# Interleaved column orders for the moving operand and the accumulator of 3,210 matmuls

## The chip, the cores and the metric

The kernel runs on one core of one Trainium2 chip. The metric is the device time of one execution in microseconds (us). TensorE (PE in the profile) multiplies, VectorE (DVE) and ScalarE (ACT) prepare operands and empty accumulators, GpSimd (POOL) and SyncE (SP) issue transfers. SBUF holds the operands, and PSUM holds the accumulators in banks of 512 fp32 columns for each of 128 partitions.

## The reference: one attention layer between two norms

With 256 rows and a width of 4096, one layer is computed:

```
h   = x + (o * silu(g)) @ w_out          # w_out: 4096 x 4096
q,k,v,g = split(rms_norm(x, norm_attn) @ w_in, 4)   # w_in: 4096 x 16384
o   = stick_breaking_attention(q, k, v)  # 32 heads of 128, strictly causal
out = rms_norm(h, final_norm)
```

All of it is float32. The weights have 5 x 4096 x 4096 values, 335 MB.

## The kernel before

**Arithmetic.** A float32 product is made of three matmuls in the type fp32r: each operand is cut into a rounded high part and the low rest, and `mm3` (L762) issues high by high, high by low and low by high into one accumulator. The rows (x, later the gated heads) are the stationary operand: 128 x 128 blocks `sh`/`sl` and, in the second projection, `oh`/`ol`. The weights are the moving operand: tiles `wh` (made by ACT) and `wl` (made by DVE), 512 columns wide, straight from the loaded tile `raw`.

**Units and steps.** The work is cut into 20 units, one after the other. Units 0 to 15 make the first projection, units 16 to 19 the second. Each unit goes through 16 steps along the width, and keeps seven accumulators b1 to b7 of 128 x 512 in seven PSUM banks. A unit from 1 on uses sums of blocks so that a step needs seven products in place of eight: steps 1, 3, 4, 6, 7, 9, 10, 12, 13 and 14 are such seven-product steps (`SEVEN`, L42, `SEVEN_PARTS`, L73), the other six have eight (`EIGHT_PARTS`, L79). So a unit has 10 x 7 + 6 x 8 = 118 products, or 354 matmuls. An eight-product step goes through the accumulators in the order 2, 2, 4, 4, 5, 5, 3, 3. The last step of a unit and the first of the next are both of that kind.

**Emptying the accumulators.** When a unit ends, `combine` (L658) makes the four results of the unit, in the tiles `qk_sb` and `gv_sb`. ACT copies b1 (L681, L682), DVE adds b6 and b7 (`add`, L665), then DVE adds b2, b4, b5 (twice) and b3 with a factor for each row (`add_scaled`, L668: one instruction SCALAR_TENSOR_TENSOR on 512 columns). An accumulator that has been read is given back (`nc.give`), and the next unit's first product into that bank waits for it.

**Order of the instructions.** The order on each engine is not written out by hand: the class `Plan` (L102) runs a model of the engines while the kernel is built. Each piece of work has a cost (`vector_ns`, L90) and a due time (`key`); a free engine takes the waiting piece with the lowest key. A changed cost can so move later instructions on all engines. `product` (L1185) calls `mm3` with the accumulator's bank and the weight's tile.

**Beside the projections** the heads of earlier units are computed: short matmuls `tr`, `z`, `o` between the products, and work on ACT and DVE.

Of the kernel before, what the change touches and what calls it, by code (L numbers as in the profile page):

```python
# [13 lines left out]
AF = mybir.ActivationFunctionType  # L14
ALU = mybir.AluOpType
# [4 lines left out]
P = 128  # L20
# [8 lines left out]
W = 2 * CW  # L29
# [27 lines left out]
ON_SCALAR = ((1, 3, 5), (1, 3))  # L57
AHEAD, SUMS_AHEAD = 4.0, 3.0
BLOCKS_LATER = 2


PLAIN = {"C11": 1, "C21": 6, "C12": 7, "C22": 3}
# [27 lines left out]
def vector_ns(n):  # L90
    return 67 + 1.0417 * n


def scalar_ns(n):
    return 98 + n / 1.2
# [142 lines left out]
def kernel(  # L238
# [10 lines left out]
    nc = Plan(tc)  # L249
    scale = 1.0 / math.sqrt(P)  # L250
# [49 lines left out]
    for g, (n, k) in enumerate(order):  # L300
        p = parts[n]
        b = p["u"], p["prods"][k][0]
# [8 lines left out]
    def place_at(u, s):  # L311

        return place_of[u + int(s // NS), step_at(u + int(s // NS), int(s % NS))]

    def soon(c=4.0):
        return nc.here + 1e3 * c


    def dve(emit, n, key=None, **kw):
        n = n if isinstance(n, tuple) else (n,)  # L320
        cost = sum(vector_ns(m) for m in n) + 122 * (len(n) - 1)
        return nc.work("vector", cost, emit, soon() if key is None else key, **kw)

    def act(emit, n, key=None, **kw):
        n = n if isinstance(n, tuple) else (n,)
        cost = sum(scalar_ns(m) for m in n) + 100 * (len(n) - 1)
        return nc.work("scalar", cost, emit, soon() if key is None else key, **kw)
# [14 lines left out]
    def together(*works):  # L342
        for w in works:
            nc.start(w)
# [164 lines left out]
    def blocks_of(i):  # L509
# [38 lines left out]
        nc.tell(("form", "s", i))  # L548
        later = place_at(0, i + BLOCKS_LATER)
        if not i:  # L550
# [19 lines left out]
    for k in range(WARM):  # L570
# [10 lines left out]
        out=bound, in_=bound, compare_op=ALU.is_gt, fill=0.0, base=0,  # L581
# [6 lines left out]
        out=tri_f, in_=tri_f, compare_op=ALU.is_ge, fill=0.0, base=0, pattern=[[-1, P]], channel_multiplier=1,  # L588
# [66 lines left out]
        yield dve(lambda: nc.vector.tensor_copy(neg_tri, tri_f), P)  # L655


    def combine(u, one, two, what):  # L658

        bank = ev[u]  # L660
        key = place_of[u + 1, 0]

        row = [rs["v"][:, t : t + 1] if u < OUT0 else 1.0 for t in range(NT)]

        def add(to, b, f, n):  # L665
            return dve(lambda: nc.vector.tensor_tensor(out=to, in0=bank[b], in1=f, op=ALU.add), W, key + n)

        def add_scaled(to, b, f, n, t):  # L668
            if u >= OUT0:
                return add(to, b, f, n)  # L670
            return dve(
                lambda: nc.vector.scalar_tensor_tensor(
                    out=to, in0=bank[b], scalar=row[t], in1=f, op0=ALU.mult, op1=ALU.add
                ),
                W, key + n,
            )

        def scaled(to, f, t):
            return act(lambda: nc.scalar.activation(to, f, AF.Copy, scale=row[t]), W, key - 2e3)

        yield act(lambda: nc.scalar.copy(two[:, 0, :], bank[1]), W, key - 2e3)  # L681
        yield scaled(one[:, 0, :], bank[1], 0)  # L682
        nc.give("b1")

        def early():
            yield nc.until(("full", u, 6))
            yield add(two[:, 0, :], 6, two[:, 0, :], 0)
            nc.give("b6")
            yield nc.until(("full", u, 7))
            yield add(two[:, 1, :], 7, two[:, 0, :], 0)  # L690
            nc.give("b7")
            yield scaled(one[:, 1, :], two[:, 1, :], 1)
            if u < OUT0:
                for t in (1, 0):
                    yield scaled(two[:, t, :], two[:, t, :], t)
            nc.tell(("early", u))

        def first_():
            yield nc.until(("full", u, 2))
            yield add_scaled(one[:, 0, :], 2, one[:, 0, :], 1, 0)  # L700
            nc.give("b2")
            yield nc.until(("full", u, 4), ("early", u))
            yield add_scaled(one[:, 1, :], 4, one[:, 1, :], 2, 1)
            nc.give("b4")
            nc.tell((what[0], u))

        def second():
            yield nc.until(("full", u, 5), ("early", u))
            for t in (1, 0):
                yield add_scaled(two[:, t, :], 5, two[:, t, :], 3, t)  # L710
            nc.give("b5")
            yield nc.until(("full", u, 3))
            yield add_scaled(two[:, 0, :], 3, two[:, 0, :], 4, 0)
            nc.give("b3")
            nc.tell((what[1], u))

        together(early(), first_(), second())

    def out_of(u):

        if u < 1:
            yield nc.until(("full", u, PLAIN["C11"]), "factor")
        else:
            yield nc.until(("full", u, 1))
        yield nc.take("one", "two")
        one = st["qk", u] = ap.tile([P, NT, W], F32, tag="one", name=f"qk_sb{u}")
        two = st["gv", u] = ap.tile([P, NT, W], F32, tag="two", name=f"gv_sb{u}")
        if u >= 1:
            yield from combine(u, one, two, ("qk", "gv"))
            return  # L730
        key = place_of[u + 1, 0] - 2e3
        for dst, col, t in ((one, 1, 0), (one, 1, 1), (two, 2, 0), (two, 2, 1)):
            b = PLAIN[f"C{t + 1}{col}"]
            yield nc.until(("full", u, b))
            yield act(
                lambda: nc.scalar.activation(dst[:, t, :], ev[u][b], AF.Copy, scale=rs["v"][:, t : t + 1]), W, key
            )
            nc.give(f"b{b}")
            if t == 1:
                nc.tell((("qk", "gv")[col - 1], u))  # L740


    st, ev = {}, {}
# [15 lines left out]
        nc.give("qkl")  # L759
        nc.tell(("gate", u))  # L760

    def mm3(out_, a, b, start, stop):  # L762

        (ah, al), (bh, bl) = a, b
        kw = dict(skip_group_check=True)
        nc.tensor.matmul(out_, ah, bh, start=start, stop=False, **kw)
        nc.tensor.matmul(out_, ah, bl, start=False, stop=False, **kw)
        nc.tensor.matmul(out_, al, bh, start=False, stop=stop, **kw)
# [195 lines left out]
    class Rows:  # L964


        def __init__(self, c):
            self.c = c

        def __getitem__(self, at_):  # L970
            return hs[self.c, at_[1]]
# [72 lines left out]
    def mixed_h(u, c):  # L1044
        yield nc.until(("full", u, 1))
        if c == NJ - 4:
            yield nc.take("raw", "gh")
        for k in range(2):
            new_h(c + k)
        yield from combine(u, Rows(c), Rows(c + 1), ("C1", "C2"))  # L1050
        yield nc.until(("C1", u), ("C2", u))
        nc.tell(("C", u))
# [132 lines left out]
    def product(n, k):  # L1185
        p = parts[n]
        b, f, c = p["prods"][k]
        h, l = forms[p["s"]]
        mm3(
            ev[p["u"]][b],  # L1190
            (h[:, PLACES[f], :], l[:, PLACES[f], :]),
            (wh[n][:, c, :], wl[n][:, c, :]),
            starts[p["u"], b] == (n, k),
            ends[p["u"], b] == (n, k),
        )

    def products():
        for g, (n, k) in enumerate(order):
            p = parts[n]
            u, s = p["u"], p["s"]  # L1200
            b, f, c = p["prods"][k]
            if u < 1:
                what = "s"
            elif u < OUT0:
                what = "n"
            elif u == OUT0:
                what = "o"
            else:
                what = "r" if u == LAST and s in EIGHT_LAST else "p"
            if starts[u, b] == (n, k):  # L1210
                yield nc.take(f"b{b}")
                ev.setdefault(u, {})[b] = acc.tile([P, W], F32, tag=f"b{b}", name=f"acc{u}_{b}")
            yield nc.until(("low", n, c), ("form", what, s), lead=nc.LEAD)
            yield nc.work(
                "tensor", PRODUCT, lambda: product(n, k), g * PRODUCT, after=lambda n=n, k=k: done(n, k), hold=False
            )
            nc.here = g * PRODUCT
# [59 lines left out]
```

## Time and profile before

| | |
|---|---|
| median of 2 runs | 1740.36 us (1740.18 to 1740.54) |
| span of the profiled execution, first to last instruction | 1738.8 us |
| between the span and the median, before the first and after the last instruction | 1.6 us |
| PE, DVE, ACT, POOL busy in the span | 1722.9, 1643.5, 1204.9, 335.5 us |
| granted TensorE clock, mean | 0.998 |
| matmuls of the projections | 7,149 |

A line of the profile names the engine, the operation, the tiles written and read (out<-in), shape and count, then the busy time, the mean duration of one, and how long the engine was idle before. All instructions go through one recording helper, so that every line is L121 and the tiles tell them apart. A matmul's duration overlaps the next one's; how fast a row of matmuls goes is read from the distance of their starts. A row of the view by windows gives, for a stretch of time, its length, the busy time of PE, of its weight load, of DVE, ACT and POOL, the granted clock, the share of the DMA engines and GB/s.

### The profile page before, as it was taken

How to read it: one execution, taken by the hardware profiler on the slowest of the kernel's cores; microseconds unless marked ns; L12 is line 12 of the kernel's file. 1: busy time of each engine (PE TensorE's matmuls, PEld its weight loads, DVE VectorE, ACT ScalarE, POOL GpSimd, SP SyncE). 2: the span in 40 equal slices, each digit the busy share in tenths (PEclk: the TensorE clock that was granted, in tenths of full speed). 3: DMA queues.
4: the chain of work that ended last, by engine and by line, in shares of the span. 5: the costliest groups of instructions: out<-in, count | busy, mean ns of one | idle time of the engine just before them, and what ended most of it. 6: DMA issues, size and time to landing. Idle time of an engine off the chain costs nothing.

```text
span 1738.8 us, 24830 instructions
## 1 busy us (share of the span) xinstructions
PE 1722.9 (99%) x7735; PEld 1412.5 (81%) x7735; DVE 1643.5 (95%) x2106; ACT 1204.9 (69%) x1640; POOL 335.5 (19%) x407
## 2 busy tenths in 40 slices
PE   9999999999999999999999999999999999999997
PEld 6888888888888888888888888888888888878885
DVE  8889999999999999999999999999999987999997
ACT  7976767676767676767676767676767675666655
POOL 0022222222222221212222222222222112221220
PEclk9999999999999999999999999999999999999999
DMA  9967788878787878787878787878787878788895
GB/s 363 297 191 227 229 231 226 230 229 236 224 234 223 240 216 238 217 251 208 255 206 255 206 256 198 257 203 259 198 256 203 269 245 265 230 268 251 233 303 191
DMA packets 249380, 413.79 MB, mean 238 GB/s; under 512 B 28128, under 2 KB 73440, under 8 KB 249248
## 3 DMA queue, kind: packets, MB, share of 16 engines
q1 hardware_dynamic: 194544, 354.24, 60.6%
q0 software_dynamic: 54416, 57.70, 20.2%
q8 instruction: 60, 0.98, 0.2%
q14 instruction: 72, 0.59, 0.1%
q10 hardware_dynamic: 288, 0.28, 0.0%
HBM read 403.98 MB, written 8.13 MB: 237 GB/s over the span
## 4 chain that ended last, share of the span: by engine, by line
PE 78%; DVE 12%; issue 6%; ACT 2%; DMA 2%; SPq 0%; DVEq 0%; ACTq 0%
PE acc L121 74%; DVE wl L121 8%; DVE raw L121 3%; PE z L121 2%; PE o L121 1%; ACT wh L121 1%; DMA raw<-in_w_in_dram 1%; PE tr L121 1%; DVE gv_sb L121 1%; DVE h L121 0%; DMA raw<-in_w_out_dram 0%; DMA grow<-in_gain_out_dram 0%; DVE qk_sb L121 0%; SPq L121 0%; ACT sq L121 0%
## 5 line engine op out<-in xcount | busy, mean ns | idle before, releaser
L121 ACT CAST wh<-raw 128x1024 fp32r<-128x1024 f32 (+1 forms) x995 | 922.0, 971 | 406.1 <-issue 180.0
L121 DVE TENSOR_TENSOR wl<-raw,wh 128x1024 fp32r<-128x1024 f32 (+1 forms) x995 | 1068.8, 1123 | 58.4 <-ACT wh L121 56.6
L121 PE MATMUL acc<-wh,sh 128*128 128x512 f32 x1898 | 755.6, 398 | 0.0
L121 PE MATMUL acc<-wl,sh 128*128 128x512 f32 x1898 | 740.0, 390 | 0.8 <-DVE wl L121 0.8
L121 PE MATMUL acc<-wh,sl 128*128 128x512 f32 x1898 | 740.5, 390 | 0.0
L121 POOL DMA_DIRECT2D raw<-in_w_in_dram x300 | 262.9, 988 | 1078.9 <-DMA raw<-in_w_in_dram 427.4
L121 PEld LDWEIGHTS acc<-wh,sl 128*128 128x128 f32 x1898 | 356.3, 188 | 75.8 <-DVE sl L121 0.4
L121 PEld LDWEIGHTS acc<-wl,sh 128*128 128x128 f32 x1898 | 357.0, 188 | 73.8 <-DVE wl L121 2.8
L121 PEld LDWEIGHTS acc<-wh,sh 128*128 128x128 f32 x1898 | 356.8, 188 | 70.7 <-ACT wh L121 0.6
L121 DVE TENSOR_TENSOR raw<-raw,raw 128x512 f32<-128x512 f32 x354 | 243.4, 687 | 6.9 <-DMA raw<-in_w_out_dram 1.2
L121 PE MATMUL acc<-wl,oh 128*128 128x512 f32 x485 | 189.7, 391 | 2.0 <-DVE wl L121 1.8
L121 PE MATMUL acc<-wh,oh 128*128 128x512 f32 x485 | 190.0, 392 | 0.0
L121 PE MATMUL acc<-wh,ol 128*128 128x512 f32 x485 | 188.9, 389 | 0.0
L121 DVE TENSOR_TENSOR raw<-raw 128x512 f32<-128x512 f32 x177 | 121.0, 684 | 0.0
L121 PEld LDWEIGHTS acc<-wl,oh 128*128 128x128 f32 x485 | 91.1, 188 | 23.8 <-DVE wl L121 5.3
L121 PEld LDWEIGHTS acc<-wh,oh 128*128 128x128 f32 x485 | 91.0, 188 | 19.2 <-DVE gv_sb L121 0.5
L121 PEld LDWEIGHTS acc<-wh,ol 128*128 128x128 f32 x485 | 91.0, 188 | 18.8
L121 POOL DMA_DIRECT2D raw<-in_w_out_dram x54 | 47.1, 968 | 185.9 <-DVE wl L121 58.9
L121 ACT ACTIVATE f<-f 128x384 f32<-128x384 f32 x96 | 50.5, 526 | 3.0
L121 ACT COPY qkT<-tr 128x512 f32<-128x512 f32 x32 | 18.6, 581 | 24.1 <-PE tr L121 24.1
L121 ACT CAST oh<-p 128x512 fp32r<-128x512 f32 (+3 forms) x46 | 20.9, 467 | 18.8 <-DVE p L121 13.2
L121 DVE SCALAR_TENSOR_TENSOR gv_sb<-acc,rin_v,gv_sb 128x512 f32<-128x512 f32 x45 | 33.4, 741 | 0.0
(91 smaller groups left out, 750.3 us busy)
## 6 DMA issues: line engine op xcount, KB each, us to landing
raw<-in_w_in_dram SPq DMA_DIRECT2D x1024, 256.0 KB, 4.5
raw<-in_w_out_dram SPq DMA_DIRECT2D x256, 256.0 KB, 4.3
raw<-in_w_in_dram POOLq DMA_DIRECT2D x300, 128.0 KB, 4.7
p<-spill POOLq DMA_DIRECT2D x28, 256.0 KB, 4.2
raw<-in_w_out_dram POOLq DMA_DIRECT2D x54, 128.0 KB, 5.1
xr<-in_x_dram SPq DMA_DIRECT2D x16, 256.0 KB, 4.8
xres<-in_x_dram SPq DMA_DIRECT2D x16, 256.0 KB, 5.6
out_dram<-h SPq DMA_DIRECT2D x16, 256.0 KB, 2.8
```

The source lines that it names most:

```text
L121: return self.tc.keep_in_program_order(getattr(self.engine, name)(*args, **kw))
```

## The change

`walked(t, (h, e))` reads the 512 columns of a tile as h blocks of runs of e neighbouring columns, and takes run 0 of every block, then run 1 of every block, and so on: (4, 2) goes through columns 0 1, 128 129, 256 257, 384 385, 2 3, 130 131 and so on. Between two runs lie 512 / h columns.

- In units 2, 3 and 4, six steps each (1, 3, 6, 9, 12, 14) take moving operand and accumulator in the same such order, so that every column ends where it ended before. `combine` of these units stays as it was.
- In units 6, 8, 10 and 12 only the accumulator is written in such an order; in units 7, 9, 11 and 13 only the moving operand is read in it. Then the columns stand in PSUM in another order than in the result, and `combine` puts them back: its copies and adds take one operand in the interleaved order, and `add_scaled` becomes four instructions on 128 columns (two on 256 for the order (16, 16)).

```diff
+WALKS = {
+    (u, s): w
+    for u, ws in {
+        2: ((4, 2), (8, 2), (16, 2), (32, 2), (64, 2), (128, 2)),
+        3: ((8, 4), (16, 4), (32, 4), (64, 4), (4, 8), (8, 8)),
+        4: ((16, 8), (32, 8), (4, 32), (8, 32), (32, 4), (64, 4)),
+    }.items()
+    for s, w in zip((1, 3, 6, 9, 12, 14), ws)
+}
+OUT_WALKS = {6: (32, 4), 8: (8, 16), 10: (16, 16), 12: (64, 2)}
+IN_WALKS = {7: (32, 4), 9: (8, 16), 11: (16, 16), 13: (64, 2)}
+def walked(t, w):
+    return t.rearrange("p (h i e) -> p i h e", h=w[0], e=w[1]) if w else t
+def cut_like(t, w):
+    i = W // w[0] // w[1] if w else 1
+    return t.rearrange("p (i h e) -> p i h e", i=i, e=w[1]) if w else t
...
+    class Banks:
...
+        def __getitem__(self, b):
+            u = self.u
+            ow, iw = OUT_WALKS.get(u), IN_WALKS.get(u)
+            return walked(ev[u][b], ow) if ow else cut_like(ev[u][b], iw)
     def combine(u, one, two, what):
-        bank = ev[u]
+        ow, iw = OUT_WALKS.get(u), IN_WALKS.get(u)
+        bank = Banks(u)
+        side = lambda t: walked(t, iw) if iw else cut_like(t, ow)
...
         def add_scaled(to, b, f, n, t):
             if u >= OUT0:
                 return add(to, b, f, n)
-            return dve(
-                lambda: nc.vector.scalar_tensor_tensor(
-                    out=to, in0=bank[b], scalar=row[t], in1=f, op0=ALU.mult, op1=ALU.add
-                ),
-                W, key + n,
-            )
+            if not ow and not iw:
...
+            def pieces():
+                T, B, F = side(to), bank[b], side(f)
+                for i in range(T.shape[1]):
+                    nc.vector.scalar_tensor_tensor(
+                        out=T[:, i], in0=B[:, i], scalar=row[t], in1=F[:, i], op0=ALU.mult, op1=ALU.add
+                    )
+            return dve(pieces, (P,) * 4, key + n)
...
-    def mm3(out_, a, b, start, stop):
+    def mm3(out_, a, b, start, stop, to=None, by=None):
         (ah, al), (bh, bl) = a, b
+        out_, bh, bl = walked(out_, to), walked(bh, by), walked(bl, by)
+        if to and not by:
+            bh, bl = cut_like(bh, to), cut_like(bl, to)
+        if by and not to:
+            out_ = cut_like(out_, by)
```

`product` hands `mm3` the order of its unit and step for the accumulator and for the moving operand.

More of the change, by code (lines that the diff above doesn't have):

```diff
@@ L655, in constants, with __init__ @@
         yield dve(lambda: nc.vector.tensor_copy(neg_tri, tri_f), P)
+    class Banks:
+        def __init__(self, u):
+            self.u = u
+        def __getitem__(self, b):
+            u = self.u
+            ow, iw = OUT_WALKS.get(u), IN_WALKS.get(u)
+            return walked(ev[u][b], ow) if ow else cut_like(ev[u][b], iw)
     def combine(u, one, two, what):
-        bank = ev[u]
+        ow, iw = OUT_WALKS.get(u), IN_WALKS.get(u)
+        bank = Banks(u)
+        side = lambda t: walked(t, iw) if iw else cut_like(t, ow)
         key = place_of[u + 1, 0]
@@ L665, in add @@
         def add(to, b, f, n):
-            return dve(lambda: nc.vector.tensor_tensor(out=to, in0=bank[b], in1=f, op=ALU.add), W, key + n)
+            return dve(lambda: nc.vector.tensor_tensor(out=side(to), in0=bank[b], in1=side(f), op=ALU.add), W, key + n)
         def add_scaled(to, b, f, n, t):
@@ L670, in add_scaled, with scaled @@
                 return add(to, b, f, n)
-            return dve(
-                lambda: nc.vector.scalar_tensor_tensor(
-                    out=to, in0=bank[b], scalar=row[t], in1=f, op0=ALU.mult, op1=ALU.add
-                ),
-                W, key + n,
-            )
[L678 to L682, printed above, removed]
+            if not ow and not iw:
+                return dve(
+                    lambda: nc.vector.scalar_tensor_tensor(
+                        out=to, in0=bank[b], scalar=row[t], in1=f, op0=ALU.mult, op1=ALU.add
+                    ),
+                    W, key + n,
+                )
[4 more added lines that the diff above has]
+                        out=T[:, i], in0=B[:, i], scalar=row[t], in1=F[:, i], op0=ALU.mult, op1=ALU.add
+                    )
+            return dve(pieces, (P,) * 4, key + n)
+        def scaled(to, f, t, side=lambda t: t):
+            return act(lambda: nc.scalar.activation(side(to), f, AF.Copy, scale=row[t]), W, key - 2e3)
+        yield act(lambda: nc.scalar.copy(side(two[:, 0, :]), bank[1]), W, key - 2e3)
+        yield scaled(one[:, 0, :], bank[1], 0, side)
         nc.give("b1")
@@ L1194, in product @@
             ends[p["u"], b] == (n, k),
+            WALKS.get((p["u"], p["s"]), OUT_WALKS.get(p["u"])),
+            WALKS.get((p["u"], p["s"]), IN_WALKS.get(p["u"])),
         )
```

## The prediction

> **What bounds the kernel now.** I read the page's head first, then the PE groups by shape, the timeline of PE, and the view by windows.
>
> ```profile
> span 1738.8 us, 24830 instructions
> PE 1722.9 (99%) x7735; PEld 1412.5 (81%) x7735; DVE 1643.5 (95%) x2106; ACT 1204.9 (69%) x1640; POOL 335.5 (19%) x407
> ```
>
> ```profile
> L121 PE MATMUL acc<-wh,sh 128*128 128x512 f32 x1898 | 755.6, 398 | 0.0
> L121 PE MATMUL acc<-wh,sl 128*128 128x512 f32 x1898 | 740.5, 390 | 0.0
> ...
> L121 PE MATMUL acc<-wh,oh 128*128 128x512 f32 x485 | 190.0, 392 | 0.0
> ...
> L121 PE MATMUL warm<-idle 128*128 128x512 bf16 x10 | 4.4, 628 | 1.3 <-DVE idle L121 1.3
> ```
>
> There are three products with the same counts for `sh` and three for `oh`: 3 x 1898 + 3 x 485 = 7149 projection matmuls. Their real pace is the distance of starts; 34 distances lie between these two rows:
>
> ```profile
> 704.11 0.39 PE L121 MATMUL acc<-wl,sh 128*128 128x512 f32 x1
> ...
> 711.81 0.39 PE L121 MATMUL acc<-wh,sl 128*128 128x512 f32 x1
> ```
>
> (711.81 - 704.11) / 34 = 0.2265 us a matmul. 7149 x 0.2265 = 1619 us of the span's 1738.8 us. The windows below are units 2, 6, 11 and 13, then the sum over eleven windows: units 2, 3, 4 and 6 to 13, those that the change touches.
>
> ```profile
> core 0: us, PE busy (x) PEld busy (x) DVE busy (x) ACT busy (x) POOL busy (x), PEclk, DMA share, GB/s
> 181.15:267.23 86.08, 86.08 (x392) 70.80 (x391) 82.96 (x102) 60.45 (x80) 18.15 (x22) 1.00 0.81 229
> ...
> 525.47:611.61 86.14, 86.14 (x391) 70.82 (x390) 82.98 (x103) 60.41 (x80) 17.95 (x22) 1.00 0.82 230
> ...
> 956.24:1042.34 86.10, 86.10 (x392) 70.81 (x390) 82.97 (x102) 60.46 (x80) 18.01 (x21) 1.00 0.80 229
> ...
> 1128.45:1214.54 86.09, 86.09 (x391) 70.80 (x390) 82.94 (x102) 61.41 (x81) 19.12 (x23) 1.00 0.82 233
> sum 947.33, PE 947.33 PEld 778.88 DVE 912.59 ACT 665.06 POOL 198.53; mean PE 86.12 PEld 70.81 DVE 82.96 ACT 60.46 POOL 18.05
> ```
>
> PE is busy 947.33 of 947.33 us at the full granted clock. So a nanosecond on each matmul there lengthens the kernel, one for one. The second thing to see is DVE: 82.96 of 86.12 us a unit, only 3.16 us idle.
>
> **Part 1, the matmuls.** The order of the columns changes no count and no size. Both-sided: 18 steps x 7 products x 3 = 378 matmuls. Accumulator alone: 4 units x 354 = 1416. Moving operand alone: 1416. Together 3210 of 7149. Runs of two columns are read from the moving operand in unit 2 (6 x 21 = 126) and unit 13 (354), 480 matmuls; written to the accumulator in unit 2 and unit 12, also 480; together 834.
>
> No matmul of the trace has an interleaved operand, so the price is bounded. Lower end: nothing, the 0.2265 us above. Upper end: the slowest row on 512 columns is the warm-up's 628 ns against 390, 238 ns more, about one more pass over the columns (512 columns take 0.2265 us). Below nothing the trace gives no faster row on 512 columns, and a faster PE would soon wait for DVE: 3.16 us idle a unit at most. I take nothing: pairs and longer runs stay neighbours, the pace of one column in 0.44 ns is all that the rows show, and no row shows a penalty for an address. That is the weakest step, and the range holds the rest.
>
> [...]
>
> **Part 2, DVE in units 6 to 13.** Five `add_scaled` a unit are cut into pieces.
>
> ```profile
> L121 DVE TENSOR_TENSOR wl<-raw,wh 128x512 fp32r<-128x512 f32 x179 | 122.4, 684 | 1.2 <-ACT wh L121 1.2
> L121 DVE SCALAR_TENSOR_TENSOR gv_sb<-acc,rin_v,gv_sb 128x512 f32<-128x512 f32 x45 | 33.4, 741 | 0.0
> L121 DVE TENSOR_TENSOR ol<-p,oh 128x128 fp32r<-128x128 f32 x13 | 3.7, 284 | 0.0
> ```
>
> From 684 to 284 ns: 384 columns are 400 ns. A piece of 128 takes 741 - 400 = 341 ns, one of 256 741 - 267 = 474. Now the end of unit 6 on DVE, then the first four products of unit 7 into b2, b4, b5 and b3 (six matmuls each) on PE:
>
> ```profile
> 609.12 0.74 DVE L121 SCALAR_TENSOR_TENSOR qk_sb<-acc,rin_v,qk_sb 128x512 f32<-128x512 f32 x1
> 609.77 1.82 DVE L121 TENSOR_TENSOR wl<-raw,wh 128x1024 fp32r<-128x1024 f32 x2
> 611.51 0.68 DVE L121 TENSOR_TENSOR raw<-raw,raw 128x512 f32<-128x512 f32 x1
> 612.11 0.74 DVE L121 SCALAR_TENSOR_TENSOR qk_sb<-acc,rin_v,qk_sb 128x512 f32<-128x512 f32 x1
> 612.77 0.74 DVE L121 SCALAR_TENSOR_TENSOR gv_sb<-acc,rin_v,gv_sb 128x512 f32<-128x512 f32 x1
> 613.43 0.68 DVE L121 TENSOR_TENSOR raw<-raw,raw 128x512 f32<-128x512 f32 x1
> 614.03 0.74 DVE L121 SCALAR_TENSOR_TENSOR gv_sb<-acc,rin_v,gv_sb 128x512 f32<-128x512 f32 x1
> 614.69 0.68 DVE L121 TENSOR_TENSOR raw<-raw 128x512 f32<-128x512 f32 x1
> 615.29 0.74 DVE L121 SCALAR_TENSOR_TENSOR gv_sb<-acc,rin_v,gv_sb 128x512 f32<-128x512 f32 x1
> ```
>
> ```profile
> 611.61 0.39 PE L121 MATMUL acc<-wh,sh 128*128 128x512 f32 x1
> ...
> 613.33 0.47 PE L121 MATMUL acc<-wh,sh 128*128 128x512 f32 x1
> ...
> 615.26 0.58 PE L121 MATMUL acc<-wh,sh 128*128 128x512 f32 x1
> ...
> 616.83 0.40 PE L121 MATMUL acc<-wh,sh 128*128 128x512 f32 x1
> ```
>
> Neighbours on DVE overlap by 0.09 us (609.12 + 0.74 against 609.77), so a whole add occupies 0.65 us. Four pieces occupy 4 x 0.251 = 1.00 us if they overlap as well, 4 x 0.341 = 1.36 if not: 0.35 to 0.71 us more. Two pieces: 0.12 to 0.30 more. A unit has five: 1.8 to 3.6 us in six units, 0.6 to 1.5 in two. Against 3.16 us idle this just about fits, so the sum of DVE work isn't on the path; its moment is. b5 is released at 614.03 + 0.74 = 614.77, and PE wants it at 615.26: 0.49 us to spare. Ahead of that release stand four adds, which bring 4 x 0.35 to 0.71 = 1.4 to 2.8 us. The planner, which books four pieces at 1.17 us in place of 0.60, moves one of the two sums `raw` from ahead of the release to behind it: 0.60 us less. The release comes at 615.6 to 617.0, PE waits 0.3 to 1.7 us. b3 follows with one sum (0.60) and one add (1.0 to 1.4), at 617.2 to 619.0, against 616.83 plus that wait: 0.1 to 0.4 us more. What is queued behind on DVE are the next step's sums and `wl` tiles, up to 2 us later; PE has up to five pairs of tiles ahead, and by its own wait gains on neither. So 0.4 to 2.1 us a unit, and I take 1.0, near the overlapping end, since the pieces touch different columns and the order of the changed kernel shows no wait between most of them. Six units: 6 us. The two-piece units: 4 x 0.12 to 0.30 less the 0.60 moved, 0 to 0.6; I take none.
>
> **Part 3, the rest.** The two TENSOR_TENSOR adds and the ACT copies of b1 keep their sizes and take one interleaved operand; I price this at nothing, as their columns come at 1.04 ns on DVE (400 / 384), slower than PE's. ACT has 86.12 - 60.46 = 25.7 us a unit to cover it; DVE has no such cover (below). The transfers on SP and POOL keep their number and order; PE's matmuls are the same, with the heads' short groups a few products away.
>
> **Sum.** 1738.8 + 6 = 1744.8 us of span, and the 1.6 us between span and median (1740.36) make 1746 us. With the ends of part 2 it is 1742 to 1755.
>
> **Rivals.**
>
> R1, the other side: a run of two columns is too short for the moving operand's read, and each such matmul takes a second pass. For it: PE's read at 0.44 ns a column is the fastest stream of the trace, more than twice DVE's 1.04. Against it: nothing in the trace. 480 x 0.238 = 114 us: 1860 us. It passes 2% (35 us) from 73 ns a matmul on. Units 2 and 13 alone get longer, unit 13 by 84 us.
>
> R2: runs of two are slow in the accumulator, alone or as well: units 2 and 12. Alone 1860 again; with R1 834 x 0.238 = 198 us: 1945.
>
> R3: any interleaving costs, whatever the run. At 238 ns for all 3210 that is 764 us: 2510; a tenth of it, 24 ns, gives 1823. [...] Against it: runs of 16 and 32 columns leave most neighbours as they were. [...]
>
> R4: DVE reads interleaved columns slower. If the seven adds of a unit took twice their 0.6 us, some 4.4 us a unit come to part 2's 1.8 to 3.6, 3 to 5 over the idle 3.16. When DVE was short of idle time, PE lost some:
>
> ```profile
> 1500.00:1540.00 40.00, 39.00 (x171) 31.62 (x170) 39.94 (x48) 25.14 (x33) 8.91 (x11) 1.00 0.83 242
> 1600.00:1640.00 40.00, 39.07 (x170) 31.36 (x169) 39.83 (x46) 26.34 (x35) 9.88 (x12) 1.00 0.88 263
> ```
>
> Eight units x 4 = 32 us at most: 1746 to 1778, about 1768.
>
> R5: the interleaved orders are faster, by a pace that the straight order hides. DVE's idle time less part 2 leaves about 1 us a unit: some 1735.
>
> **How the numbers follow.** Forecast (no cost on PE) 0.45, R4 0.06, R5 0.03, R1 0.22, R2 0.10, R3 0.14. A measurement of this kernel can tell about 2%, 35 us, from no change. Forecast, R5 and most of R4 lie within it: 0.53. R1, R2 and R3 lie above it, but for small prices: 0.46. More than 2% faster has no room: 0.01. The range goes from R5 (1735) to R1 and R2's single form with the ends of part 2 (1870), and leaves out R2's double form and most of R3, 0.18 or so. The forecast's own range is 1741 to 1760.
>
> **What would show it.** In the profile of the changed kernel: the distance of starts in units 2, 12 and 13, 0.2265 us if I am right and up to 0.46 under R1 or R2, and each of the eighteen steps by itself; the same in units 6 to 11 under R3. The group SCALAR_TENSOR_TENSOR 128x128 near 341 ns, x4 a unit's add. PE waits for b5 at the ends of units 6 to 9, 12 and 13, about 1 us each. I am wrong if a pace other than 0.2265 us holds through a whole unit, or if DVE runs without idle time there.

## The result: 1861.42 us, and the profile after

| | before | after |
|---|---|---|
| median of 2 runs | 1740.36 us | 1861.42 us (1860.66 to 1862.18) |
| ratio, 95% interval | | 1.0696 (1.0665 to 1.0727) |
| span of the profiled execution | 1738.8 us | 1860.5 us |
| granted TensorE clock | 0.998 | 0.998 |

The kernel became 7.0% slower, by 121 us. That is the 1860 us of rival R1, and 115 us over the forecast. The head of the page of the changed kernel (all its instructions stand at L143, where they stood at L121):

```profile
span 1860.5 us, 24938 instructions
PE 1843.7 (99%) x7735; PEld 1425.4 (77%) x7735; DVE 1660.4 (89%) x2206; ACT 1206.9 (65%) x1640; POOL 334.7 (18%) x407
```

PE has the same 7735 matmuls and is busy 1843.7 - 1722.9 = 120.8 us longer: the whole difference is matmul time. The view by windows shows where. Its rows are units 2, 3, 9, 11, 12 and 13, each from its first matmul to that of the next unit, and then the sum over all of units 2, 3, 4 and 6 to 13:

```profile
core 0: us, PE busy (x) PEld busy (x) DVE busy (x) ACT busy (x) POOL busy (x), PEclk, DMA share, GB/s
180.70:295.58 114.88, 114.88 (x391) 73.65 (x390) 86.23 (x104) 62.55 (x80) 19.73 (x24) 1.00 0.65 179
295.58:383.22 87.64, 87.64 (x392) 71.45 (x391) 82.55 (x101) 61.02 (x79) 16.44 (x20) 1.00 0.77 218
...
814.59:904.75 90.16, 90.16 (x392) 71.56 (x391) 85.79 (x120) 60.17 (x80) 18.07 (x21) 1.00 0.79 221
...
991.18:1081.42 90.24, 90.24 (x392) 71.31 (x391) 84.81 (x110) 60.26 (x80) 18.32 (x22) 1.00 0.78 223
1081.42:1167.81 86.39, 86.34 (x392) 70.92 (x390) 82.53 (x106) 59.40 (x78) 16.89 (x20) 1.00 0.79 222
1167.81:1335.67 167.86, 167.86 (x391) 78.32 (x390) 90.96 (x130) 63.35 (x81) 20.97 (x25) 1.00 0.46 125
sum 1069.01, PE 1068.71 PEld 791.48 DVE 931.10 ACT 668.15 POOL 201.50; mean PE 97.16 PEld 71.95 DVE 84.65 ACT 60.74 POOL 18.32
```

The sum grew by 1069.01 - 947.33 = 121.7 us. Unit 2 grew by 28.8 us (86.08 before) and unit 13 by 81.8 us (86.09 before): 110.6 of it. These two read runs of two columns from the moving operand. Unit 12, which writes runs of two into the accumulator, grew by 0.3 us. Units 9 and 11 (moving operand, runs of 16) grew by 4.1 us each and unit 3 by 1.6 us. In unit 13 PE is busy without a gap while the DMA share falls from 0.82 to 0.46: it waits for nobody, its matmuls are slow. The timeline of PE in unit 13, five distances of starts between the rows:

```profile
1247.35 0.66 PE L143 MATMUL acc<-wh,sh 128*128 128x512 f32 x1
...
1249.65 0.66 PE L143 MATMUL acc<-wh,sl 128*128 128x512 f32 x1
```

(1249.65 - 1247.35) / 5 = 0.460 us. The same in unit 12, eighteen distances:

```profile
1139.90 0.39 PE L143 MATMUL acc<-wh,sh 128*128 128x512 f32 x1
...
1143.98 0.39 PE L143 MATMUL acc<-wh,sh 128*128 128x512 f32 x1
```

4.08 / 18 = 0.2267 us, the pace of before. The same run of two columns costs 0.460 - 0.227 = 0.233 us more, a whole second pass, on the side that is read and nothing on the side that is written.

The groups of DVE by shape, for part 3, and the ACT copy of b1:

```profile
L143 DVE TENSOR_TENSOR gv_sb<-acc,gv_sb 128x512 f32<-128x512 f32 x30 | 20.5, 683 | 6.4 <-PE acc L143 6.4
L143 DVE SCALAR_TENSOR_TENSOR gv_sb<-acc,rin_v,gv_sb 128x128 f32<-128x128 f32 x72 | 20.1, 340 | 1.6 <-issue 1.6
```

```profile
L143 ACT COPY gv_sb<-acc 128x512 f32<-128x512 f32 x15 | 8.7, 582 | 0.5 <-PE acc L143 0.5
```

683 ns for an add on 512 columns is what a straight one took in the prediction (684), and a piece of 128 takes 340 ns where 341 was worked out. The adds and the copies here are those of all units, straight and interleaved. In units 6 to 13 alone the adds take 681 to 692 ns (679 to 686 before) and the copies 574 to 590 (570 to 583 before), with one copy of 627 in unit 13. So R4 falls: but for that copy, interleaved columns cost DVE and ACT at most some 10 ns each.

### The profile page after: what moved, and what is told of

The parts are those of the page before. It is cut to its first block, busy times and chain, and to the rows that moved or that the text cites. A ratio compares the mean times of both kernels' runs of the same rounds, so it can differ in the third digit from the quotient of the medians.

```text
span 1860.5 us, 24938 instructions
## 1 busy us (share of the span) xinstructions
PE 1843.7 (99%) x7735; PEld 1425.4 (77%) x7735; DVE 1660.4 (89%) x2206; ACT 1206.9 (65%) x1640; POOL 334.7 (18%) x407
## 4 chain that ended last, share of the span: by engine, by line
PE 81%; DVE 9%; issue 4%; DMA 3%; ACT 2%; SPq 0%; DVEq 0%; POOL 0%; ACTq 0%; POOLq 0%
PE acc L143 77%; DVE wl L143 6%; DMA raw<-in_w_out_dram 2%; PE z L143 2%; DVE raw L143 2%; ACT wh L143 1%; PE o L143 1%; PE tr L143 1%; DMA grow<-in_gain_out_dram 0%; DMA raw<-in_w_in_dram 0%; DVE gv_sb L143 0%; DVE h L143 0%; SPq L143 0%; DVE qk_sb L143 0%; ACT xs L143 0%
## 5 line engine op out<-in xcount | busy, mean ns | idle before, releaser
L143 ACT CAST wh<-raw 128x1024 fp32r<-128x1024 f32 (+1 forms) x995 | 922.3, 971 | 455.6 <-PE acc L143 244.2
L143 DVE TENSOR_TENSOR wl<-raw,wh 128x1024 fp32r<-128x1024 f32 (+1 forms) x995 | 1074.4, 1123 | 126.1 <-ACT wh L143 120.5
L143 PE MATMUL acc<-wh,sh 128*128 128x512 f32 x1898 | 800.9, 422 | 0.1
L143 PE MATMUL acc<-wl,sh 128*128 128x512 f32 x1898 | 785.4, 414 | 0.7 <-DVE wl L143 0.7
L143 PE MATMUL acc<-wh,sl 128*128 128x512 f32 x1898 | 785.7, 414 | 0.0
L143 POOL DMA_DIRECT2D raw<-in_w_in_dram x300 | 262.3, 982 | 1179.7 <-DMA raw<-in_w_in_dram 508.5
L143 PEld LDWEIGHTS acc<-wh,sl 128*128 128x128 f32 x1898 | 360.0, 190 | 112.6 <-issue 40.4
L143 PEld LDWEIGHTS acc<-wl,sh 128*128 128x128 f32 x1898 | 360.2, 190 | 106.0 <-issue 34.6
L143 PEld LDWEIGHTS acc<-wh,sh 128*128 128x128 f32 x1898 | 360.0, 190 | 105.9 <-issue 37.1
L143 DVE TENSOR_TENSOR raw<-raw,raw 128x512 f32<-128x512 f32 x354 | 243.1, 687 | 6.5 <-DMA raw<-in_w_out_dram 1.7
L143 PE MATMUL acc<-wl,oh 128*128 128x512 f32 x485 | 189.6, 391 | 2.8 <-DVE wl L143 2.6
L143 PE MATMUL acc<-wh,oh 128*128 128x512 f32 x485 | 189.9, 392 | 0.1
L143 PE MATMUL acc<-wh,ol 128*128 128x512 f32 x485 | 188.9, 389 | 0.0
L143 DVE TENSOR_TENSOR raw<-raw 128x512 f32<-128x512 f32 x177 | 121.0, 684 | 0.0
L143 PEld LDWEIGHTS acc<-wl,oh 128*128 128x128 f32 x485 | 91.1, 188 | 24.6 <-DVE wl L143 6.1
L143 PEld LDWEIGHTS acc<-wh,oh 128*128 128x128 f32 x485 | 91.1, 188 | 19.0 <-DVE gv_sb L143 0.5
L143 PEld LDWEIGHTS acc<-wh,ol 128*128 128x128 f32 x485 | 91.1, 188 | 18.9
L143 POOL DMA_DIRECT2D raw<-in_w_out_dram x54 | 47.0, 968 | 188.8 <-DMA raw<-in_w_out_dram 58.3
L143 ACT ACTIVATE f<-f 128x384 f32<-128x384 f32 x96 | 50.5, 526 | 3.0
L143 ACT COPY qkT<-tr 128x512 f32<-128x512 f32 x32 | 18.7, 585 | 52.0 <-PE tr L143 52.0
L143 DVE SCALAR_TENSOR_TENSOR gv_sb<-acc,rin_v,gv_sb 128x128 f32<-128x128 f32 (+2 forms) x105 | 40.9, 436 | 1.6 <-issue 1.6
L143 ACT ACTIVATE a<-z 128x384 f32<-128x384 f32 x32 | 15.7, 490 | 40.4 <-PE z L143 38.0
```

The lines of the kernel that those rows point to most:

```text
L143: return self.tc.keep_in_program_order(getattr(self.engine, name)(*args, **kw))
```

## The experiments

R1 gave the time, but it had no reason beyond "too short". The experiments ask what makes a run short, what the rest of the 121 us is, and whether anything beats the straight order.

**Every order, one after the other.** The kernel before, with another order in single steps of units 1 to 15, from step 8 to step 14 (21 matmuls, or 24 in steps 8 and 11); most orders touch the moving operand alone, five the accumulator alone, four both. Two estimates stood against each other: theory N (what counts is the length of a run of neighbouring columns: two cost double, single columns more, four or more nothing) and theory L (the columns come in lines of 16 bytes, four fp32 columns, and each change of a line costs 226.5 / 128 = 1.77 ns).

```diff
-    def mm3(out_, a, b, start, stop):
+    def mm3(out_, a, b, start, stop, c, by, to):
...
+        if by:
+            bh, bl = read_in(bh, c, by), read_in(bl, c, by)
...
+        if to:
+            out_ = read_in(out_.rearrange("p (k n) -> p k n", k=1), 0, to)
```

> The kernel before, with single steps of units 1 to 15 in one column order each: in most only the moving operand is read in another order, in five only the accumulator is written so, in four both. Columns are not put back in place and are read several times in some orders, so the output is not the reference's; counts and sizes of all matmuls stay. Theory L (lines): the moving operand comes in 16-byte lines of four fp32 columns, each turn to another line costs the time of four columns in the straight order (226.5 / 128 = 1.77 ns), never less than some 227 ns a matmul. Theory N (neighbours): what counts is the length of a run of neighbouring columns; runs of two cost double, single columns more, runs of four or more nothing, wherever they lie. Pace in ns, L / N: order 0 2 1 3 within each four: 227 / 450 or more; runs of four that begin two columns into a line: 453 / 227; every second column, then the others: 453 / 900; single columns from 128 to 4 blocks: 907 by both; first two of each four read twice: 227 / 453; first four of sixteen read four times: 227 or less / 227; one column 512 times: 227 or less / 900; runs of two from odd columns: 680, half of them cross a line / 453; straight from column 1 or 2 on: 227 by both. Runs of two in the accumulator alone: 227 by both; 300 or more if an accumulator must be contiguous.

A single execution took 1892.59 us. Rows of the windows view, one step each from its first matmul to that of the next step, 21 matmuls (24 in the fourth and the fifth, since in the seven-product steps one product of seven keeps its straight beginning), in this order: single columns (128,1); runs of two (64,2); the order 0 2 1 3 within each four; runs of four that begin two columns into a line (32,4); runs of two from odd columns on (64,2); single columns (4,1); one column 512 times; and runs of two written to the accumulator alone (128,2). The columns are those of the windows above.

```profile
...
167.35:177.01 9.66, 9.66 (x22) 4.36 (x21) 6.14 (x8) 3.56 (x4) 0.00 (x0) 1.00 0.15 43
380.33:390.00 9.67, 9.67 (x22) 4.36 (x21) 6.06 (x8) 3.56 (x4) 0.00 (x0) 1.00 0.15 43
750.30:755.11 4.81, 4.81 (x22) 3.96 (x21) 1.27 (x2) 2.18 (x3) 0.00 (x0) 1.00 0.01 2
718.72:729.56 10.84, 10.84 (x25) 4.97 (x24) 7.24 (x9) 3.05 (x3) 2.91 (x4) 1.00 0.79 247
816.32:827.39 11.07, 11.07 (x25) 4.99 (x24) 7.25 (x9) 3.04 (x3) 2.94 (x4) 1.00 0.72 231
...
261.11:267.05 5.94, 5.94 (x22) 4.04 (x21) 4.55 (x6) 2.62 (x3) 1.72 (x2) 1.00 0.86 240
942.00:946.53 4.53, 4.53 (x22) 3.97 (x21) 3.42 (x5) 2.34 (x3) 0.00 (x0) 1.00 0.43 164
1030.81:1035.58 4.77, 4.77 (x22) 3.94 (x21) 4.56 (x6) 2.47 (x4) 0.00 (x0) 1.00 0.64 215
...
```

9.66 / 21 is 460 ns, 4.81 / 21 is 229, 10.84 / 24 is 452, 11.07 / 24 is 461, 5.94 / 21 is 283, 4.53 / 21 is 216, 4.77 / 21 is 227. The paces of all orders, from the distances of starts, in ns a matmul, means of a step (straight: 226.7):

| moving operand | ns |
|---|---|
| single columns in 16 to 256 blocks; in 4 | 431 to 461; 283 |
| runs of two, in 4 to 128 blocks; in 2 | 431 to 487; 333 |
| runs of four, in 2, 4, 8, 16, 32, 64 blocks | 251, 267, 278, 247, 225, 233 |
| runs of eight, in 2 to 32 blocks | 231 to 250 |
| runs of 16 and 32 | 231 to 240 |
| runs of four, begun two columns into a line | 452 |
| runs of eight, begun two columns into a line | 355 |
| runs of two, begun at odd columns | 461 |
| straight, begun at column 1 or 2 | 232 to 234 |
| 0 2 1 3 within each four; first two of four read twice | 227 (median; means 228 to 230) |
| first four of 16 four times; one column 512 times | 216 |
| **accumulator alone**, runs of two in 4, 16, 32, 64 and 128 blocks | 227 (median; means 227 to 232) |
| **both**, (16,4), (32,4), (64,4), (32,8) | 246, 224 to 227, 231, 232 to 233: as the read alone |

N fell: 0 2 1 3 has no run longer than two and costs nothing, and runs of four cost 452 ns once they straddle lines. L was right there, but single columns should have cost 907 ns, twice as much as runs of two, and they cost the same; runs of two from odd columns should have cost 680 and cost 461. So a line of four fp32 columns matters (runs of four: 225 to 278 ns each in one line, 452 across two), but not simply each change of it. The accumulator takes runs of two at no price in all five spacings (median 227 ns).

**The pieces alone.** The change with all matmuls straight; `combine` still cuts its adds.

```diff
-WALKS = {
...
-OUT_WALKS = {6: (32, 4), 8: (8, 16), 10: (16, 16), 12: (64, 2)}
-IN_WALKS = {7: (32, 4), 9: (8, 16), 11: (16, 16), 13: (64, 2)}
+WALKS = {}
+OUT_WALKS = {u: (1, 256) if u in (10, 11) else (1, 128) for u in range(6, 14)}
+IN_WALKS = {}
```

> The kernel before, and of the change only the cut of the adds: in units 6 to 13 add_scaled is four instructions on 128 neighbouring columns (two on 256 in units 10 and 11); no order of columns is changed. By the prediction's part 2 PE waits about 1 us at six unit ends: 1746 us (1742 to 1755). By the changed kernel's trace, in which units 8 to 14 after such an end are 0.1 to 0.6 us longer beside what their own order costs: 1741 to 1743 us.

1743.55 us (1742.41 to 1745.40) against 1740.17: 1.0019 (1.0010 to 1.0028), +3.4 us. DVE at the end of unit 6, four pieces in a row (x4), then the first matmul of unit 7 into b5:

```profile
611.81 1.12 DVE L135 SCALAR_TENSOR_TENSOR qk_sb<-acc,rin_v,qk_sb 128x128 f32<-128x128 f32 x4
612.85 1.11 DVE L135 SCALAR_TENSOR_TENSOR gv_sb<-acc,rin_v,gv_sb 128x128 f32<-128x128 f32 x4
613.88 0.68 DVE L135 TENSOR_TENSOR raw<-raw,raw 128x512 f32<-128x512 f32 x1
614.48 1.11 DVE L135 SCALAR_TENSOR_TENSOR gv_sb<-acc,rin_v,gv_sb 128x128 f32<-128x128 f32 x4
615.52 0.68 DVE L135 TENSOR_TENSOR raw<-raw,raw 128x512 f32<-128x512 f32 x1
```

```profile
615.70 0.58 PE L135 MATMUL acc<-wh,sh 128*128 128x512 f32 x1
```

Four pieces occupy 612.85 - 611.81 = 1.04 us, one of the two sums `raw` has gone behind b5, and b5 comes free at 614.48 + 1.11 = 615.59. All of this is part 2 of the prediction, at its cheap end (615.6). The price is 0.2 to 0.5 us at each of the eight unit ends, where I took 1.0 at six of them and nothing at the two others. Of the waits of the weight load in units 6 to 13 (total, times, the longest) two are new against before, beside 1.9 us that the view puts down to no other engine:

```profile
PEld z L135 <- ACT qkT L135: 2.9, 7, 0.4
...
PEld acc L135 <- DVE gv_sb L135: 1.5, 5, 0.3
```

The second is the forecast one, an accumulator that DVE has not yet read for `gv_sb`. The first was not forecast: the planner also moved `tr` one product later (from 612.98 to 613.85 us after the end of unit 6), and `z` now waits for the `qkT` that ACT copies from it. How the 3.4 us divide between these waits is not shown.

**Without the runs of two in the read.** The change with (32, 4) in place of the runs of two on the moving operand; unit 12 keeps its runs of two in the accumulator.

```diff
-        2: ((4, 2), (8, 2), (16, 2), (32, 2), (64, 2), (128, 2)),
+        2: ((32, 4),) * 6,
...
-IN_WALKS = {7: (32, 4), 9: (8, 16), 11: (16, 16), 13: (64, 2)}
+IN_WALKS = {7: (32, 4), 9: (8, 16), 11: (16, 16), 13: (32, 4)}
```

> The changed kernel, but no moving operand is read in runs of two: unit 2's six steps and unit 13 take the order (32, 4). The accumulator of unit 12 is still written in runs of two. Theories L and N both: unit 13 loses its 82 us and unit 2 its 29 us, 1861 - 111 = 1750 us. If the runs of two were not the cause but that unit 13 and unit 2 interleave at all, or the neighbours' work: it stays above 1800 us.

1751.89 us (1751.04 to 1752.85) against 1740.17: 1.0068 (1.0052 to 1.0083), +11.7 us. Its page:

```profile
span 1749.7 us, 24938 instructions
PE 1733.3 (99%) x7735; PEld 1414.6 (81%) x7735; DVE 1654.7 (95%) x2206; ACT 1202.7 (69%) x1640; POOL 334.5 (19%) x407
```

PE is busy 1843.7 - 1733.3 = 110.4 us less than in the changed kernel. So 110 of the 121 us are the 480 matmuls that read runs of two, shown by taking them out. (In unit 2 the edit takes them out of the accumulator too; the scan has the same reads alone at the same price.) Of the 11.7 left, units 3, 9 and 11 make 9.8 (1.6, 4.1 and 4.1): there runs of four, eight or sixteen are read from blocks of some spacings at 231 to 278 ns. The rest, some 2 us, is left for the pieces, which took 3.4 when alone.

**The cheapest order everywhere.** In the scan (32, 4) came out at 224 to 227 ns. Is that a gain over 226.7, or an accident?

```diff
+WALKS = {(u, s): (32, 4) for u in range(20) for s in range(16)}
+OUT_WALKS, IN_WALKS = {}, {}
```

> The kernel before, with moving operand and accumulator of every projection matmul in the order (32, 4), so that every column ends in its place and combine stays as before. If the pace of 223 ns in steady steps of units 3 and 4 of the changed kernel holds against 226.7: 3.4 ns x 354 = 1.2 us a unit less, within DVE's 3.16 us idle, some 18 us in units 1 to 15 and less where DVE is short: 1720 us. If that pace is an accident of those steps (the moving side alone in unit 7 has a mean of 226.7 with single distances of 220 to 239): 1740 us. Slower than 1745 would say that some engine's reads get in its way.

1738.22 us (1735.87 to 1740.70) against 1740.17: 0.9989 (0.9980 to 0.9998). Most steps go at 226 to 227 ns, some at 223. R5 has no more than that in this order.

**Lines in turn, and bf16.** The second scan took single columns in turn from few lines, in the same steps, and in place of the warm-up nine rows of 14 bf16 matmuls on a tile of zeros.

```diff
+    if kind == "turned":
+        return w.rearrange("p (k h e) -> p k e h", h=spec[1], e=spec[2])
```

> The kernel before, with single steps of units 1 to 5 whose moving operand alone is read in another order (three steps for each of seven orders; columns are not put back, so the output is not the reference's), and ahead of the work nine series of 14 bf16 matmuls on zeros, which nothing uses. In the first scan single columns from far blocks cost 431 to 461 ns, no more than runs of two, and single columns from 4 blocks 283; so neither turns times 1.77 ns (907) nor runs hold. Theory G (groups): columns are read four at a time; a group costs 1.67 ns if its lines are those of the group before, 1.77 with one fresh line, 3.4 to 3.8 with two or more. Theory T (turns): each turn to another line costs 0.9 ns when a single column is read between turns, however soon the line comes again. All seven orders are single columns, 512 turns: T says 431 to 461 for each. G: columns in turn from 2 neighbouring lines, (0 4 1 5) (2 6 3 7): 333; from 2 rows of eight columns: 333; from 2 blocks of 256: 333; from 4 neighbouring lines: 280; from 8 or 16 neighbouring lines, and from 8 blocks of 64, where a line comes again only after another group: 431 to 490. bf16, moving operand straight and in runs of 8, 4, 2, 1: if a group is four columns 216, 216, 227, 453, 461; if it is 16 bytes, eight columns: 216, 216, 227, and 231 for runs of 2. bf16, accumulator in runs of 2, 64 blocks: 216; single columns from 64 and 256 blocks: 216 if writes don't mind, 430 if it is written two columns at a time.

A single execution took 1823.21 us. Windows of 21 matmuls: single columns in turn from two neighbouring lines (0 4 1 5 2 6 3 7), from four lines, from eight lines:

```profile
183.80:188.33 4.53, 4.53 (x22) 3.98 (x21) 3.83 (x6) 2.59 (x3) 0.00 (x0) 1.00 1.02 260
...
188.33:193.96 5.63, 5.63 (x22) 3.99 (x21) 5.63 (x7) 3.38 (x5) 1.71 (x2) 1.00 0.84 206
199.44:209.50 10.06, 10.06 (x22) 4.37 (x21) 7.00 (x9) 3.56 (x4) 0.00 (x0) 1.00 0.37 127
```

That is 216, 268 and 479 ns. Two lines in turn go *faster* than the straight order, which neither G (333 ns) nor T (431 to 461) had; both fell, though G came near on four lines (280) and on the bf16 reads. The bf16 rows, 14 matmuls between the bounds of each: runs of eight, four, two and one column read, then runs of two and of one written to the accumulator:

```profile
core 0: us, PE busy (x), PEclk, DMA share, GB/s
8.41:11.43 3.02, 3.02 (x16) 1.00 1.05 398
11.43:14.59 3.16, 3.16 (x15) 1.00 1.05 392
14.59:20.90 6.31, 6.31 (x16) 1.00 1.05 387
20.90:27.22 6.32, 6.32 (x15) 1.00 0.23 81
...
30.48:33.50 3.02, 3.02 (x14) 1.00 0.00 0
33.67:39.68 6.01, 6.01 (x16) 1.00 0.00 0
```

216, 226, 451 and 451 ns read; 216 and 429 ns written.

This made theory H, an estimate worked out from the paces of the two scans. By it the columns go in pairs, one pair in 0.84 ns (216 ns for 256). The first of each pair belongs to one stream and the second to another, and each stream holds one 16-byte line. A new line costs its stream about 1.77 ns (226.5 / 128), however many columns it takes from it. A stream that takes one column from each line goes at 256 x 1.77 = 453 ns. Two columns a line give half, 227 ns. Four or more give the 216 ns of the pairs. In the straight fp32 order the first stream takes columns 0, 2, 4, 6: two a line, so even the order of before pays 11 ns (226.7 against 216). Runs of two give each stream one column a line (431 to 487 ns measured), and so do single columns from many blocks (431 to 461), runs of four that straddle (452) and odd runs of two (461). 0 2 1 3 gives two (227). In bf16 the 16 bytes of a line would be eight columns: four a stream in runs of eight (216 measured), two in runs of four (226), one in runs of two (451). The rows named here come out within some 8%, and 0 4 1 5 gives four a stream and its 216; runs of four from blocks of some spacings do not (up to 278 where H has 227). H is a fit to the two scans, made after them. No later run tries an order that they had not timed, so the streams themselves are argued and not shown.

**H used for a gain.** The kernel before, its moving operand read as 0 4 1 5 2 6 3 7. The weights' columns are laid out beforehand so that the accumulator stays as it was.

```diff
+        bh, bl = (t.rearrange("p (k h e) -> p k e h", h=2, e=4) for t in (bh, bl))
+        out_ = out_.rearrange("p (k e h) -> p k e h", h=2, e=4)
...
-        return w.reshape(NS, KT, P, n, CW).transpose(3, 0, 2, 1, 4)
+        w = w.reshape(NS, KT, P, n, CW // 8, 4, 2).swapaxes(-1, -2).reshape(NS, KT, P, n, CW)
+        return w.transpose(3, 0, 2, 1, 4)
```

> The kernel before, with two edits. TensorE reads each eight columns of the moving operand in the order 0 4 1 5 2 6 3 7, and the host lays the weights' columns so that this order is the old one; the accumulator is written straight, as before, and nothing else changes. Theory H, formed on the second scan: the columns are read in pairs, the first of each pair by one stream and the second by another; each stream holds one 16-byte line, and a fresh line takes a stream 1.77 ns however many columns it takes from it. Straight order: two columns of each line, 128 x 1.77 = 227 ns; runs of two or less: one, 453; this order: four, so that only the pairs' own 0.83 ns count, 216 ns. H expects 216 ns in all projection matmuls. PE's unit falls from 86.1 to 82.3 us, below DVE's 82.96, which becomes the bound: some 83 to 83.5 us a unit, 15 x 2.8 = 42 us, and up to 8 us in units 0 and 16 to 19: 1690 to 1700 us. If 216 is a pace of those few steps that doesn't hold for all, or if DVE, ACT or the loads already hold the end: 1735 to 1740.

1731.89 us (1731.53 to 1733.07) against 1740.76: 0.9948 (0.9935 to 0.9962). It beats both kernels, by 8.9 us over the one before, and not by the 40 to 50 expected. The timeline of PE, seventeen distances:

```profile
561.29 0.38 PE L121 MATMUL acc<-wl,sh 128*128 128x512 f32 x1
...
564.96 0.38 PE L121 MATMUL acc<-wh,sh 128*128 128x512 f32 x1
```

3.67 / 17 = 0.216 us: the pace is as H says. The page and the window of unit 6 show why the time is not:

```profile
span 1730.2 us, 24832 instructions
PE 1665.6 (96%) x7735; PEld 1417.9 (82%) x7735; DVE 1640.9 (95%) x2106; ACT 1200.9 (69%) x1640; POOL 334.5 (19%) x407
```

```profile
520.19:606.12 85.93, 83.37 (x391) 71.03 (x390) 82.89 (x102) 60.38 (x81) 18.67 (x22) 1.00 0.80 232
```

PE's busy time fell by 57.3 us and the span by 8.6. A unit still takes 85.93 us where PE is busy 83.37. Its waits in that window, total, times and the longest, and then those of DVE:

```profile
PE acc L121 <- DVE wl L121: 1.1, 2, 0.7
PE z L121 <- DVE fl L121: 0.8, 2, 0.5
...
```

```profile
DVE wl L121 <- ACT wh L121: 2.5, 5, 0.6
DVE f L121 <- ACT f L121: 0.2, 1, 0.2
```

PE now waits for DVE. DVE is busy 82.89 us and waits 2.7 us for ACT, 85.6 of the unit's 85.93: it sums `raw`, ACT makes `wh` from the sum, and DVE needs `wh` for `wl`. The waits of unit 6 before the change are the same two rows, 2.5 and 0.2 us. So most of the 3.16 us that I called idle was already taken by this round trip. That DVE with it is the bound is read from these rows; no run here removes the round trip. Of the 8.6 us, unit 0 alone gives 4.0 (85.72 us where it took 89.75) and unit 1 gives 1.3; each of units 2 to 13 gives 0.1 to 0.4.

**The same, with the planner told.** The planner's model of a matmul lowered to the new pace.

```diff
-    return 0.4167 * n + 13.4 if n > 128 else 109.0
+    return 0.4167 * n + 2.6 if n > 128 else 109.0
```

> As p4_turned, and the planner books a matmul of 512 columns at 216 ns in place of 226.7, so that due times and the order of the instructions follow the faster pace. If the order planned for the slower pace costs p4_turned some waits: up to 5 us below p4_turned. If DVE's work is the bound alone: the same within 2 us. If tighter due times push the emptying of accumulators behind other work: slower by some us.

1738.00 us (1736.38 to 1739.53) against 1740.76: 0.9984 (0.9975 to 0.9993), some 6 us slower than without it. Unit 6 takes 86.51 us here. DVE is busy 82.58 of them and waits for ACT 2.3 us with `wl` and 1.4 with `f`: 86.3 us together. So DVE with its waits for ACT fills the unit again, and with the new due times `f` waits 1.4 us where it waited 0.2.

## Why the prediction was wrong, point by point

- **What bounds the kernel: right.** PE was busy throughout, and a nanosecond on each matmul came through one for one: 120.8 us of PE, 121 us of time.
- **Part 1, the price of nothing: this step failed.** "Pairs and longer runs stay neighbours" isn't what counts. That this makes them free was not shown: no row of the trace before had an interleaved operand, and in the scan reads in runs of two took 431 to 487 ns in 4 to 128 blocks. For 480 matmuls that read runs of two the price is 110.6 / 480 = 230 ns, 3% from the upper end of 238 ns. That the warm-up's row is so near is luck: the 238 ns compared durations (628 and 390), and the warm-up read straight columns. By H, the estimate, a stream that takes one column from each line takes just twice the 227 ns. The price of nothing was right for the accumulator (1416 matmuls alone, among them all of unit 12) and for runs of four in the spacing (32, 4). For the moving operand in units 9 and 11 it was wrong by 13 ns (240 against 227), some 4 us a unit.
- **Part 2: right in mechanism, too dear.** Moved sum, late b5 and the small wait came as described; 3.4 us in all where I took 6. The wait of `z` for `qkT`, which may be a part of it, I did not have.
- **Part 3: right.** 683 ns an add, 582 a copy. But "DVE only 3.16 us idle" was not free time, as the turned order showed.
- **Rivals.** R1's place and price are what happened: units 2 and 13, unit 13 by 81.8 us where 84 was given. The time lies in the range of 1735 to 1870 us only because the range took R1 in. Its reason is not right as it stands: the length of a run is not what makes a read slow, since single columns in the order 0 4 1 5 go at 216 ns and runs of four that straddle lines at 452. No row of the trace before spoke for or against the price, and 0.22 was a low chance for it. R2 is wrong (unit 12: +0.3 us). R3 holds in the small, for the moving operand alone, some 10 us with unit 3. R4 and R5 fell for these orders.

**What stays open.** H doesn't say why the spacing of blocks matters: eight blocks are dearest (278 ns in runs of four, 487 in runs of two), 32 blocks cheapest (225 and 431). Nor does it give the price when a stream goes back and forth between two lines: 283 ns for (4,1), 268 for four lines, 333 for (2,2), between its 216 and 453. It is low for straight reads begun at column 1 or 2 (227; measured 232 to 234) and for runs of eight begun two columns into a line (192 lines, 340; measured 355). The first is worth some 10 us of the 121 here, in units 3, 9 and 11.

## What to carry to other kernels

In these runs the price of an order of columns did not follow the length of a run: 0 4 1 5 2 6 3 7 went at 216 ns, runs of four across lines at 452. The estimate H fits most of the paces: take every second column of the order and count how many lie together in a line of four fp32 columns (four: 216 ns, two: 227, one: 431 to 487). Here it was cheap to reorder on the accumulator's side (runs of two at 227 ns, the straight pace) and on DVE and ACT (at most some 10 ns an add or a copy, but for one copy), and dear to break the lines of the moving operand; the spacing of whole lines still cost something (224 to 278 ns in runs of four). Before a busy engine is made faster, add to the next engine's busy time the waits that stay: here that sum, 82.89 + 2.7 us of the unit's 85.93, and not the busy time alone, was where the gain ended.

## What had not been expected of the hardware

- The straight fp32r order isn't the fastest read: 226.7 ns for 512 columns, 216 in the order 0 4 1 5 2 6 3 7, as for runs of eight in bf16.
- One column read 512 times goes at 216 ns, against 226.7 straight, so that repeating a column cost nothing.
- The accumulator takes runs of two at full pace (227 ns in fp32, 216 in bf16) and single columns at half of it (429 ns in bf16).
- Four pieces of 128 columns follow each other on DVE at 1.04 / 4 = 0.26 us, though each takes 340 ns.
